# Gates and norm sums by quarters of the tokens, an up projection written in another order, later merges and a root on ScalarE

## The chip, the core and the metric

The kernel runs on one core of one Trainium2 chip. A core has several engines that run at the same time, each through its own list of instructions: TensorE (PE in the profile, with PEld for its weight loads), VectorE (DVE), ScalarE (ACT), GpSimd (POOL) and SyncE (SP), whose queue issues most of the transfers (DMA) here. PE multiplies and accumulates into PSUM, in banks of 128 partitions by 512 f32 numbers. The metric is the device time of one execution in microseconds (us), as the median of several runs.

## The reference, cut to what matters

One layer of a decoder for 1024 tokens and 1024 channels: a first norm, one input projection for two mixers (a gated delta rule with a causal convolution, and dilated window attention), the output projection, a second norm, a gated MLP with a causal convolution, and a last norm.

```python
def rmsnorm(x, w):
    xf = x.astype(jnp.float32)
    y = xf * lax.rsqrt(jnp.mean(xf * xf, axis=-1, keepdims=True) + EPS)
    return (y * w.astype(jnp.float32)).astype(x.dtype)
...
    h = rmsnorm(x, norm1_w)
    proj = h @ w_in
    qkv_a, z_a, b_a, a_a, qkv_b = (...)
    beta = jax.nn.sigmoid(b_a)
    g = -jnp.exp(a_log) * jax.nn.softplus(a_a + dt_bias)
    o_a = gated_delta_rule(qa, ka, va, g, beta)     # unit lower triangular solves of 64 x 64
    o_b = dilated_attention(qb, kb, vb)
    x = x + jnp.concatenate([o_a, o_b], axis=-1) @ w_out
    h = rmsnorm(x, norm2_w)
    u = causal_dwconv(h @ w_up, ffn_conv_w)
    gate, up = u[..., :D_FF], u[..., D_FF:]         # D_FF = 2816
    x = x + (jax.nn.silu(gate) * up) @ w_down
    return rmsnorm(x, final_norm_w)
```

`b_a` and `a_a` are the eight columns of the projection that hold the gates (four heads each). A norm's root is one number for each token; the kernel multiplies with it behind a product, so a product can run before the root is known.

## The kernel before

All large tensors lie transposed: channels on the 128 partitions, tokens along the free axis. A factor of a product is split into a high part (`hi`, rounded) and the rest (`lo`), and a product of two such factors is three matmuls, hi by hi, lo by hi and hi by lo (`mm3`, line 204). One of them is 128 x 128 weights by 512 tokens.

The order of PE's instructions is the order in which the program calls `mm` (line 191), which stamps each with a running number. That order is made by a small planner, `Weave` (lines 26 to 120). It holds a modelled clock of PE and a modelled time at which each tile is ready. The stages are generators with a rank; each yields the time that it would have to wait, and the planner runs the first in rank whose time has come. `wv.need(tile, slack=s)` is the modelled wait for that tile, lengthened by `s` us; `next_bank` is the same for a bank of PSUM. Where no stage of higher rank is due, the next split product of the projections (25 tiles of 16 split products beside the first 48) fills the place. The other engines follow the order in which the program issues to them, within what a scheduler rearranges by priority and by the `after(...)` lines, which only set an order; `uv` is VectorE with high priority.

The stages that the change touches:

- `first` (line 359), the first product: three tiles of keys, 48 split products, as the eight channel tiles of x arrive. `norms` (373) and `gates` (399) are woven into it. `acc` holds the squares of x summed over the channel tiles; eight matmuls with `ones` sum it over partitions, a column for each 128 tokens. VectorE scales the sums and GpSimd raises them to the power -1/2 (`rsqrt`, 239), giving `rst`. Transposes on PE (line 196) spread it over all partitions, and VectorE copies it into `rstdB`. The gates: `wba`, the weights of the eight gate columns padded to 32, is used in two batches of eight matmuls over 512 tokens, in which the channel tile modulo 4 sets one of four column groups of PE. ScalarE copies the rows into `barow`, and eight matmuls with the selection matrix `sel` add the four groups and turn the tokens to partitions. In the trace an f32 matmul leaves two records.
- `forward_sub` and `merges` (715): the inverses of the triangular matrices. VectorE makes blocks of 32 by substitution, which go through memory (`xdram`) into block-diagonal tiles `x`; `merges` joins them to 64 and 128 with small matmuls of `x` with `um`, two pairs of heads one after the other.
- the up projection (`up`, line 1300): 22 tiles, each with seven block products P1 to P7 of a Strassen kind, four split products each (k = 0 to 3). The factors are blocks of weights (A11, S1 to S4, A12, A22; two of them in one `pair`) and of activations (B11, T1 to T4, B21, B22, one for each k). P1, P6, P7 and P4 accumulate in one bank, `pa`; between them ScalarE copies it out (`p1`, `u2`, `u3`), and the product behind must wait for the copy. In the first tile `before` is None: there `rms2_power` (1226) sums the squares of the second norm, held in `rstdB` by then, with eight matmuls with `ones`. `up_weights` (1252) splits the weights of the next tiles.
- `final_norm` (1579), called for three pieces of the tokens; its last call has `more`, squares that join late. Scaling on VectorE and the power on GpSimd stand between its sums and its spread.

## Time and profile before

| what | number |
|---|---|
| median of three runs | 1202.09 us (1201.26 to 1202.52) |
| profiled execution | 1200.62 us |
| its span, first to last instruction | 1198.7 us |
| around the span | 1.92 us |
| granted TensorE clock, mean | 0.997 |
| VectorE, ScalarE, GpSimd busy | 964.7, 572.8 and 53.1 us |
| read and written in memory | 117.68 and 38.03 MB |

The stages follow each other in the span: the first product and gates up to about 45 us, projections with the delta rule and the attention to 467 us, the output projection to 555 us, the up projection to 977 us, the down projection to 1187 us, and the last norm. In a row of the timeline the first number is the start in us, the second the duration or, for a group of equal instructions, the time from the first start to the last end; then engine, line, operation, output and inputs, shapes and count, and in brackets how long the engine had been idle and what ended that. The durations of PE's rows overlap, since matmuls are pipelined: the pace is read from the starts. In a row of windows come the stretch, its length, busy time and count of PE, PEld, VectorE, ScalarE and GpSimd, and then the granted clock, the share of the DMA engines and GB/s.

### The profile page before, as it was taken

Reading aid. Unit: us, or ns where it says so; the run is one execution under the profiler, and the core shown is the slowest. Engines: PE = TensorE matmul, PEld = TensorE weight load, DVE = VectorE, ACT = ScalarE, POOL = GpSimd, SP = SyncE. Lnnn points to the kernel's source line nnn. Section 1 sums busy time; section 2 is a strip of 40 time slices with the busy share of each in tenths; the row PEclk is TensorE's granted clock in tenths of the full one; section 3 lists DMA queues with packets and bytes.
Section 4 is the critical chain, followed back from the end, with each engine's and each line's share of the span. In section 5 each row is a group of like instructions: output and inputs, shape, how many; then the busy total and the mean of one; then the engine's idle time right before and its main releaser. Section 6 shows DMA issues by size and latency. Waiting matters only on the chain.

```text
span 1198.7 us, 18255 instructions
## 1 busy us (share of the span) xinstructions
PE 1186.9 (99%) x6994; PEld 981.9 (82%) x6994; DVE 964.7 (80%) x1540; ACT 572.8 (48%) x1121; POOL 53.1 (4%) x50
## 2 busy tenths in 40 slices
PE   9999999999999999999999999999999999999997
PEld 7888888898777778888888888888888888888887
DVE  7686996484577787777898988989888889898987
ACT  7383343363343444555454544445454454445452
POOL 0212001014000000000000000000000000000001
PEclk9999999999999999999999999999999999999999
DMA  7323356737543314443223223131322396356724
GB/s 237 106 75 103 106 138 160 213 105 209 170 127 105 98 37 126 164 147 117 74 69 104 82 77 106 53 106 55 104 87 71 100 378 215 114 181 219 242 98 158
DMA packets 114664, 156.91 MB, mean 131 GB/s; under 512 B 54512, under 2 KB 65552, under 8 KB 114576
## 3 DMA queue, kind: packets, MB, share of 16 engines
q1 hardware_dynamic: 113856, 155.21, 40.7%
q8 instruction: 55, 0.90, 0.3%
q10 hardware_dynamic: 720, 0.53, 0.1%
q14 instruction: 33, 0.27, 0.1%
HBM read 117.68 MB, written 38.03 MB: 130 GB/s over the span
## 4 chain that ended last, share of the span: by engine, by line
PE 91%; DVE 3%; DMA 2%; ACT 2%; issue 1%; SPq 1%; POOL 0%; DVEq 0%; ACTq 0%; POOLq 0%
PE ps L192 41%; PE pa L192 20%; PE dw L192 17%; PE pc L192 10%; PE ps L201 1%; PE ps L196 1%; DMA vdram<-vT 1%; SPq L139 1%; DVE vT L139 1%; DMA xdram<-xi 1%; ACT sm L141 1%; DMA wst<-in_wu 0%; PE warm L192 0%; DMA vtok<-vdram 0%; DVE x1h L139 0%
## 5 line engine op out<-in xcount | busy, mean ns | idle before, releaser
L192 PE MATMUL dw<-pr 128*128 128x512 f32 (+1 forms) x984 | 211.4, 376 | 0.0
L192 PEld LDWEIGHTS dw<-pr 128*128 128x128 f32 x984 | 176.7, 188 | 33.7
L192 PE MATMUL ps<-xhi,whi 128*128 128x512 f32 x448 | 184.7, 412 | 0.0
L192 PE MATMUL ps<-xhi,wlo 128*128 128x512 f32 x448 | 175.6, 392 | 0.0
L192 PE MATMUL ps<-xlo,whi 128*128 128x512 f32 x448 | 175.5, 392 | 0.0
L192 PE MATMUL pa<-T,pair 128*128 128x512 f32 x528 | 127.1, 390 | 0.2
L192 PEld LDWEIGHTS pa<-T,pair 128*128 128x128 f32 x528 | 98.9, 188 | 21.2 <-ACT u L139 0.7
L192 PEld LDWEIGHTS ps<-xhi,whi 128*128 128x128 f32 x448 | 84.9, 189 | 19.7 <-issue 3.6
L192 PEld LDWEIGHTS ps<-xhi,wlo 128*128 128x128 f32 x448 | 84.5, 189 | 18.5
L192 PEld LDWEIGHTS ps<-xlo,whi 128*128 128x128 f32 x448 | 84.8, 189 | 14.5
L139 ACT ACTIVATE u<-pa 128x512 f32<-128x512 f32 x44 | 26.3, 599 | 109.7 <-PE pa L192 109.7
L139 DVE SCALAR_TENSOR_TENSOR y<-xu,fcw,y 128x1023 f32<-128x1023 f32 (+1 forms) x44 | 56.3, 1280 | 24.4 <-ACT y L139 24.4
L139 ACT ACTIVATE pr<-wd 128x1024 fp32r<-128x1024 f32 x33 | 35.0, 1060 | 74.6 <-DVE wd L139 36.9
L139 ACT ACTIVATE whi<-wst 128x1024 fp32r<-128x1024 f32 (+2 forms) x38 | 38.5, 1013 | 56.3 <-PE ps L192 47.1
L192 PE MATMUL pa<-B,A 128*128 128x512 f32 x264 | 63.5, 389 | 0.0
L192 PE MATMUL pa<-T,S 128*128 128x512 f32 x264 | 63.4, 389 | 0.0
L192 PE MATMUL pc<-T,S 128*128 128x512 f32 x264 | 63.4, 389 | 0.0
L192 PE MATMUL pc<-B,pair 128*128 128x512 f32 x264 | 63.4, 389 | 0.0
L139 DVE TENSOR_TENSOR wst<-wst 128x512 f32<-128x512 f32 x88 | 60.3, 685 | 0.7
L192 PE MATMUL ps<-B,pair 128*128 128x512 f32 x252 | 60.5, 389 | 0.0
L141 ACT ACTIVATE sm<-sm,mx 128x128 f32<-128x128 f32 (+7 forms) x64 | 35.4, 555 | 51.4 <-DVE mx L141 51.4
L192 PEld LDWEIGHTS pa<-T,S 128*128 128x128 f32 x264 | 49.5, 188 | 10.3
(243 smaller groups left out, 2238.9 us busy)
## 6 DMA issues: line engine op xcount, KB each, us to landing
wst<-in_wu SPq DMA_DIRECT2D x44, 512.0 KB, 3.7
wd<-in_wd SPq DMA_DIRECT2D x44, 512.0 KB, 4.5
wst<-in_wi SPq DMA_DIRECT2D x25, 512.0 KB, 4.0
upark<-y SPq DMA_DIRECT2D x22, 512.0 KB, 3.6
r<-upark SPq DMA_DIRECT2D x22, 512.0 KB, 9.5
wa<-in_wd SPq DMA_DIRECT2D x22, 256.0 KB, 3.0
apark<-aqkv SPq DMA_DIRECT2D x8, 512.0 KB, 4.4
wst<-in_wo SPq DMA_DIRECT2D x8, 512.0 KB, 3.6
```

What stands on the lines that cost most here:

```text
L139: return getattr(eng, op)(*a, **kw)
L141: return getattr(eng, op)(*a, **kw)
L192: tc.stamp_issue_order_token(nc.tensor.matmul(dst, lhs, rhs, start=start, stop=stop, **kw).ins, TOKEN)
L196: tc.stamp_issue_order_token(nc.tensor.transpose(dst, src, ident).ins, TOKEN)
L201: tc.stamp_issue_order_token(nc.tensor.transpose(dst, src[rows], ident[rows, rows]).ins, TOKEN)
```

## The change

The two batches of gate matmuls become one of 32: for each channel tile, each of the four column groups takes a quarter of the tokens (`by_quarter`, 256 tokens in runs of 32). So no group has to be added to another. `pick`, 32 columns with ones in column 8, adds the sum of `acc` to the same bank, and one transpose of VectorE brings gates and sum to `bat`, tokens on partitions. `barow`, its copies and `sel` are gone. The spread of the root and the decay's bank have more slack.

The second norm's sums in the up projection are formed in the same way. P2 of its first tile is issued in other pieces, and a split of the second tile's A11 is placed behind the copy `u2`. `merges` asks for its tiles with slack 4.5 in place of 2.5. In the last call of `final_norm` ScalarE makes the square root and VectorE the reciprocal; a small square root at step 20 of the down projection, `sc(mark, eps, AF.Sqrt)`, has ScalarE load the table for that there.

```diff
--- before.py
+++ after.py
@@ -233,6 +233,8 @@
     sa.dma_start(n1, I["n1"])
     mhalf = const("mhalf", [P, NCH])
     ve.memset(mhalf, -0.5)
+    eps = const("eps", [P, 1])
+    ve.memset(eps, EPS)
     phalf = const("phalf", [P, NCH])
     ve.memset(phalf, 0.5)
 
@@ -339,15 +341,15 @@
     ve.memset(ones, 1.0)
     tri = tile_(sp, [P, P], F32, "tri", "r0", 1)
     sy.dma_start(tri, I["tri"])
-    sel = const("sel", [P, 8], I["sel"])
+    pick = const("pick", [P, 32])
+    ve.memset(pick, 0.0)
+    ve.memset(pick[:, 8:9], 1.0)
     gcw = const("gcw", [P, 12, 4], I["gcw"])
     gnw = const("gnw", [P, 1], I["gnw"])
     alog = const("alog", [P, H], bass.AP(tensor=I["a_log"].tensor, offset=I["a_log"].offset, ap=[[0, P], [1, H]]))
     dtb = const("dtb", [P, H], bass.AP(tensor=I["dt_bias"].tensor, offset=I["dt_bias"].offset, ap=[[0, P], [1, H]]))
     gw2 = const("gw2", [P, 1])
     ve.tensor_scalar(gw2, gnw, 0.5, None, op0=OP.mult)
-    barow = A("barow", "go")
-
 
     wbank = bank("atr", "warm")
     for _ in range(10):
@@ -370,17 +372,27 @@
     rst = const("rst", [P, NCH])
     rstdB = const("rstdB", [P, S])
 
+    def by_quarter(t):
+        return t.rearrange("p (c g i) -> p g c i", g=4, i=32)
+
+    bat = sp.tile([P, NCH, 32], F32, name="bat")
+
     def norms():
+        yield wv.need(wba, xts[-1], slack=4.0)
+        pt = yield from next_bank("atr", wba, xts[-1])
+        for k in range(KT):
+            for g in range(4):
+                o = 32 * g
+                mm(pt[o:o + 32, :256], wba[:, k, :], by_quarter(xts[k])[:, g], 0.107, k == 0, False, tile_position=(0, o))
         yield wv.need(acc, slack=8.0)
-        ssp = yield from next_bank("atr", acc)
-        for c in range(NCH):
-            mm(ssp[:, c:c + 1], acc[:, c * P:(c + 1) * P], ones[:, :1], 0.215)
-            if c % 2:
-                yield APART
-        ve.tensor_scalar(rst, ssp[:, :NCH], 1.0 / 1024, EPS, op0=OP.mult, op1=OP.add)
+        for g in range(4):
+            o = 32 * g
+            mm(pt[o:o + 32, :256], pick, by_quarter(acc)[:, g], 0.107, False, True, tile_position=(0, o))
+        uv.transpose(bat.rearrange("p c j -> p (c j)"), pt[:, :256])
+        uv.tensor_scalar(rst, bat[:, :, 8], 1.0 / 1024, EPS, op0=OP.mult, op1=OP.add)
         rsqrt(rst, rst, NCH)
         wv.done.add("rst")
-        yield wv.need(rst)
+        yield wv.need(rst, slack=4.0)
         for h in range(2):
             if h:
                 yield wv.need(rstdB, slack=0.3)
@@ -398,24 +410,9 @@
 
     def gates():
 
-        yield wv.need(wba, xts[-1], slack=4.0)
-        for h in range(2):
-            pt = yield from next_bank("atr", wba, xts[-1])
-            for k in range(KT):
-                o = 32 * (k % 4)
-                mm(pt[o:o + 32], wba[:, k, :], xts[k][:, half(h)], 0.23, k < 4, k >= 4, tile_position=(0, o))
-            ac.activation(barow[:, half(h)], pt, AF.Copy)
-            yield 2 * APART
-        yield wv.need(barow, slack=2.0)
-        pt = yield from next_bank("atr", barow)
-        for c in range(NCH):
-            mm(pt[:, c * 8:(c + 1) * 8], barow[:, c * P:(c + 1) * P], sel, 0.215)
-            if c % 2:
-                yield APART
         yield from wv.until("rst")
         ba = sp.tile([P, NCH, 8], F32, name="ba")
-        ve.tensor_tensor(ba, pt[:, :64].rearrange("p (c j) -> p c j", c=NCH),
-                                rst[:, :, None].to_broadcast([P, NCH, 8]), op=OP.mult)
+        ve.tensor_tensor(ba, bat[:, :, :8], rst[:, :, None].to_broadcast([P, NCH, 8]), op=OP.mult)
         ac.activation(beta, ba[:, :, :H], AF.Exp, scale=-1.0)
         ve.tensor_scalar(beta, beta, 1.0, None, op0=OP.add)
         ve.reciprocal(beta, beta)
@@ -431,7 +428,7 @@
         g = sp.tile([P, NCH, H], F32, name="g")
         ve.scalar_tensor_tensor(g, az, -1.0, ea[:, None, :].to_broadcast([P, NCH, H]), op0=OP.mult,
                                        op1=OP.mult)
-        pt = yield from next_bank("atr", g)
+        pt = yield from next_bank("atr", g, slack=1.5)
         g32 = g.rearrange("p c h -> p (c h)")
         mm(pt[:, :NCH * H], tri, g32, 0.215)
         mm(pt[:NCH * H, P:2 * P], g32, tri, 0.215)
@@ -739,7 +736,7 @@
             return t.rearrange("p (h c j) -> p h c j", h=2, c=NCH)
 
         w1ps = [bank(t) for t in tags]
-        yield wv.need(*w1ps, *x64s, *ys, slack=2.5)
+        yield wv.need(*w1ps, *x64s, *ys, slack=4.5)
         for h, y, x64, e in heads:
             for c in range(NCH):
                 for a, b in halves:
@@ -1211,6 +1208,7 @@
             split_block(hblock("T2", i), b11)
             split_block(hblock("B21", i), b21)
             split_block(hblock("T3", i), b12)
+            last["t3"] = last["hi"]
             ve.tensor_tensor(b21, b21, b11, op=OP.subtract)
             split_block(hblock("T4", i), b21)
             last["lasts"] = [last["hi"]]
@@ -1225,10 +1223,12 @@
 
     def rms2_power():
         ps = bank("atr")
-        for c in range(NCH):
-            mm(ps[:, c:c + 1], rstdB[:, c * P:(c + 1) * P], ones[:, :1], 0.215)
+        for g in range(4):
+            o = 32 * g
+            mm(ps[o:o + 32, :256], pick, by_quarter(rstdB)[:, g], 0.107, tile_position=(0, o))
         rs = sp.tile([P, NCH], F32, name="rs")
-        uv.tensor_scalar(rs, ps[:, :NCH], 1.0 / 1024, EPS, op0=OP.mult, op1=OP.add)
+        uv.transpose(bat.rearrange("p c j -> p (c j)"), ps[:, :256])
+        uv.tensor_scalar(rs, bat[:, :, 8], 1.0 / 1024, EPS, op0=OP.mult, op1=OP.add)
         rsqrt(rs, rs, NCH)
         return rs
 
@@ -1265,6 +1265,8 @@
                 for name in ("A11", "S2", "S1"):
                     w[name] = block(name, "Xb")
             split_block(w["A11"], g0)
+            if n == 1:
+                after(last["hi"], last["u2"], "the last channels go first")
             ve.tensor_tensor(g0, g0, u0, op=OP.subtract)
             ve.tensor_tensor(u0, u0, u1, op=OP.add)
             split_block(w["S1"], u0)
@@ -1311,21 +1313,22 @@
 
             yield from up_product(n, "P5", pc, True, False)
             pd = bank("hf", "pd")
-            yield from up_product(n, "P2", pd, ks=range(3))
+            yield from up_product(n, "P2", pd, ks=(0,))
         yield from up_product(n, "P6", pa, False, False)
         u2 = tile_(wp, [P, 512], F32, "u2", "wlo", 2)
-        inst = ac.activation(u2, pa, AF.Copy)
+        last["u2"] = inst = ac.activation(u2, pa, AF.Copy)
         if before is None:
             for hi in last["lasts"]:
                 after(hi, inst, "the next product waits for the copy")
         if before is None:
             rs = rms2_power()
+            yield from up_product(n, "P2", pd, False, False, ks=(1,))
         else:
             yield from up_product(n, "P5", pc, True, False)
         yield from up_product(n, "P7", pa, False, False)
         if before is None:
 
-            yield from up_product(n, "P2", pd, False, ks=(3,))
+            yield from up_product(n, "P2", pd, False, ks=(2, 3))
         else:
             pd = yield from next_bank("hf")
             yield from up_product(n, "P2", pd)
@@ -1586,8 +1589,12 @@
                 mm(ss[:, c:c + 1], t[:, c * P:(c + 1) * P], ones[:, :1], 0.215, i == 0 and c == 0,
                    i == len(parts) - 1, skip_group_check=True)
         rs = tile_(sp, [P, 4], F32, "rs3", "rs3", 2)
-        inst = ve.tensor_scalar(rs[:, :n_], ss[:, :n_], 1.0 / 1024, EPS, op0=OP.mult, op1=OP.add)
-        rsqrt(rs[:, :n_], rs[:, :n_], n_)
+        if more:
+            ac.activation(rs[:, :n_], ss[:, :n_], AF.Sqrt, scale=1.0 / 1024, bias=eps)
+            ve.reciprocal(rs[:, :n_], rs[:, :n_])
+        else:
+            inst = ve.tensor_scalar(rs[:, :n_], ss[:, :n_], 1.0 / 1024, EPS, op0=OP.mult, op1=OP.add)
+            rsqrt(rs[:, :n_], rs[:, :n_], n_)
         if hh:
 
             keep("vector", inst)
@@ -1663,6 +1670,8 @@
             ahead = n + 1 + (stage == 3)
             if ahead < len(STEPS):
                 prep(*STEPS[ahead], JOBS.get(n, ()))
+            if n == 20:
+                sc(mark, eps, AF.Sqrt)
             if (stage, j) == (3, HT - LAST - 2):
                 outs = final_norm(1, whole, ("hf", "ch"), lambda: down_step(stage, j))
             elif stage < 3 or j < HT - LAST:
```

PE in the first product. A row is an operation by its tiles, the shape of its output, and how many of a kind stand in a row; `ps` is a bank of PSUM, `xhi`, `xlo`, `whi` and `wlo` are the parts of x and of the weights. Before, from the second half of the sums on:

```order
L192 MATMUL ps<-ones,acc 128x1 x2
L192 MATMUL ps<-sel,barow 128x8 x2
L192 MATMUL ps<-xhi,whi 128x512
L192 MATMUL ps<-xlo,whi 128x512
L192 MATMUL ps<-xhi,wlo 128x512
L192 MATMUL ps<-ones,acc 128x1 x2
L192 MATMUL ps<-sel,barow 128x8 x2
L192 MATMUL ps<-xhi,whi 128x512
```

And after, around the sums:

```order
L192 MATMUL ps<-xhi,whi 128x512
L192 MATMUL ps<-xlo,whi 128x512
L192 MATMUL ps<-xhi,wlo 128x512
L192 MATMUL ps<-acc,pick 32x256 x4
L192 MATMUL ps<-xhi,whi 128x512
L192 MATMUL ps<-xlo,whi 128x512
L192 MATMUL ps<-xhi,wlo 128x512
```

The `sel` matmuls are gone and the sums stand in one piece. The gate batch ahead of them was two rows of 32x512 x8 and is one:

```order
L192 MATMUL ps<-xlo,whi 128x512
L192 MATMUL ps<-xhi,wlo 128x512
L192 MATMUL ps<-xt,wba 32x256 x32
L192 MATMUL ps<-xhi,whi 128x512
L192 MATMUL ps<-xlo,whi 128x512
```

It stands behind the same split product (the 22nd) as the first batch did.

PE at the merges, with the numbers of the tiles; `qT,kT` are the last products of the delta rule's preparation, `x64,um` the first of `merges`. Before:

```order
L192 MATMUL ps_1934<-qT_1772,kT_604 128x128 x4
L192 MATMUL ps_1924<-xhi_140,whi_1778 128x512
L192 MATMUL ps_1924<-xlo_141,whi_1778 128x512
L192 MATMUL ps_1924<-xhi_140,wlo_1779 128x512
L192 MATMUL ps_1734<-x64_1706,um_683 32x32 x16
L192 MATMUL ps_1734<-x64_1706,um_804 32x32 x16
```

And after:

```order
L192 MATMUL ps_1927<-xhi_155,whi_1781 128x512
L192 MATMUL ps_1927<-xlo_156,whi_1781 128x512
L192 MATMUL ps_1927<-xhi_155,wlo_1782 128x512
L192 MATMUL ps_1927<-xhi_167,whi_1781 128x512
L192 MATMUL ps_1927<-xlo_168,whi_1781 128x512
L192 MATMUL ps_1927<-xhi_167,wlo_1782 128x512
L192 MATMUL ps_1927<-xhi_179,whi_1781 128x512
L192 MATMUL ps_1927<-xlo_180,whi_1781 128x512
L192 MATMUL ps_1927<-xhi_179,wlo_1782 128x512
L192 MATMUL ps_1737<-x64_1709,um_686 32x32 x16
L192 MATMUL ps_1737<-x64_1709,um_807 32x32 x16
```

Four split products instead of one stand between them now; three of the four are shown.

PE in the first tile of the up projection, from P2 (`pd`) over P6 (`T,S`), the sums and P7 (`T,pair` into `pa`) to the start of P4. Before:

```order
L192 MATMUL pd<-B_5741,pair 128x512 x3
L192 MATMUL pa<-T_5406,S_5922 128x512 x3
L192 MATMUL pa<-T_5572,S_5922 128x512 x3
L192 MATMUL pa<-T_5738,S_5922 128x512 x3
L192 MATMUL pa<-T_5900,S_5922 128x512 x3
L192 MATMUL ps<-ones,rstdB 128x1 x8
L192 MATMUL pa<-T_5412,pair 128x512 x3
L192 MATMUL pa<-T_5578,pair 128x512 x3
L192 MATMUL pa<-T_5744,pair 128x512 x3
L192 MATMUL pa<-T_5906,pair 128x512 x3
L192 MATMUL pd<-B_5903,pair 128x512 x3
L192 MATMUL pa<-T_5416,pair 128x512 x3
```

And after:

```order
L192 MATMUL pd<-B_5412,pair 128x512 x3
L192 MATMUL pa<-T_5409,S_5925 128x512 x3
L192 MATMUL pa<-T_5575,S_5925 128x512 x3
L192 MATMUL pa<-T_5741,S_5925 128x512 x3
L192 MATMUL pa<-T_5903,S_5925 128x512 x3
L192 MATMUL ps<-rstdB,pick 32x256 x4
L192 MATMUL pd<-B_5578,pair 128x512 x3
L192 MATMUL pa<-T_5415,pair 128x512 x3
L192 MATMUL pa<-T_5581,pair 128x512 x3
L192 MATMUL pa<-T_5747,pair 128x512 x3
L192 MATMUL pa<-T_5909,pair 128x512 x3
L192 MATMUL pd<-B_5744,pair 128x512 x3
```

P2's first piece is one split product long instead of three, its second stands between the sums and P7, and the last two, of which one row is shown, stand between P7 and P4.

More of the change, by code (lines that the diff above doesn't have):

```diff
@@ L1754, in host_inputs @@
         "ident": np.eye(128, dtype=np.float32),
-        "sel": np.array([[p % 32 == j for j in range(8)] for p in range(128)], np.float32),
         "tri": (j[:, None] <= j[None, :]).astype(np.float32),
```

## The prediction

> **What bounds the kernel now.** I read the busy shares first, then the shares of the chain that ended last, then all waits of PE, then the stretches that the diff touches, engine by engine.

> ```profile
> PE 1186.9 (99%) x6994; PEld 981.9 (82%) x6994; DVE 964.7 (80%) x1540; ACT 572.8 (48%) x1121; POOL 53.1 (4%) x50
> PE 91%; DVE 3%; DMA 2%; ACT 2%; issue 1%; SPq 1%; POOL 0%; DVEq 0%; ACTq 0%; POOLq 0%
> PE ps L196 <- POOL rs L139: 1.1, 1, 1.1
> PE ps L192 <- DMA x<-xdram: 1.1, 1, 1.1
> PE ps L192 <- ACT w L141: 0.7, 2, 0.5
> PE ps L201 <- DVE sm L141: 0.6, 2, 0.3
> ```

> PE is busy 99% of the span and carries 91% of the last chain; its waits (the last four rows: total us, times, longest) are short. So time falls in two ways only: PE gets less work, or one of its few waits goes. Both kinds are in this diff. The profiled execution took 1200.62 us, of which 1198.7 is the span and 1.92 lies around it. The sums below are made against it; the median of the runs, 1202.09, is 1.47 higher, and I carry that difference over. Runs span 1201.26 to 1202.52, so 0.2% (2.4 us) is about what can be told from no change.

> **Front: gates and norm sums (gain 3.25 us).** PE has no idle time between these rows:

> ```profile
> 20.80 0.39 PE L192 MATMUL ps<-xhi,wlo 128*128 128x512 f32 x1
> 21.12 1.92 PE L192 MATMUL ps<-xt,wba 128*32 128x512 f32 x16
> 24.57 0.64 PE L192 MATMUL ps<-xt,wba 128*32 128x512 f32 x4
> 28.60 0.50 PE L192 MATMUL ps<-ones,acc 128*128 128x1 f32 x4
> 34.52 0.51 PE L192 MATMUL ps<-sel,barow 128*128 128x8 f32 x4
> 37.04 0.60 PE L196 MATMUL ps<-ident,rst 128*128 128x128 f32 x4
> 562.17 2.89 PE L192 MATMUL pa<-T,S 128*128 128x512 f32 x12
> 564.89 1.84 PE L192 MATMUL ps<-ones,rstdB 128*128 128x1 f32 x16
> ```

> The last two rows give the pace of a full 128x512 matmul: 12 of them from 562.17 to 564.89, 2.72/12 = 0.227 us, a split product of three 0.68. From the end of the product at 20.80 (21.03) to the first spread transpose at 37.04 lie 16.01 us, in which the order places 12 split products, 12 x 0.68 = 8.16. The extras are the other 7.85. From one gate batch's start to the other's are 3.45, with two split products (1.36) in between, so a batch costs 2.09 (two: 4.18); the ones and sel matmuls, each piece with its changes of kind, take the remaining 3.67.

> After, the gate batch is 32 matmuls of 256 tokens. An f32 matmul leaves two records (8 matmuls, x16), so 64 records; four column groups run side by side: the first four records of the second batch last 0.64 (its row is cut there), all 16 of the first 1.92, so a further round costs (1.92 - 0.64)/3 = 0.43, and 2.09 less 1.72 leaves 0.37 for the changes of kind. At half the width a round is 0.215 and 16 rounds are 3.44; with 0.37 they cost 3.81. The four pick matmuls are 8 records, two rounds, 0.43 + 0.37 = 0.80. Together 4.6, against 7.85: 3.25 gained. The streaming of the gates itself is not cheaper (3.44 before and after); what goes is the sel and ones work.

> The unknown is whether short records overlap as well and whether reading tokens in runs of 32 out of 128 costs.

> ```profile
> L192 PE MATMUL ps<-kT,qT 64*128 64x128 f32 x16 | 2.0, 322 | 0.0
> L192 PE MATMUL ps<-kT,qT 64*32 64x128 f32 x64 | 1.7, 269 | 0.0
> L139 DVE STREAM_TRANSPOSE vT<-vT 128x1024 f32<-128x1024 f32 x4 | 4.9, 1236 | 0.0
> 33.47 0.17 DVE L139 TENSOR_SCALAR rst<-ps 128x8 f32<-128x8 f32 x1 [1.09 <-PE ps L192]
> 33.72 1.64 POOL L139 TENSOR_TENSOR rst<-rst,mhalf 128x8 f32<-128x8 f32 x1 [32.67 <-DVE rst L139]
> ```

> The first two rows are the nearest to that: 128 tokens read strided (32 keys, 269 ns) are no longer than contiguous (322 ns). Bounds: the gain is 3.25 if all overlaps; with the 18 rounds a half longer (5.8, and 0.74) 1.3; with rounds as long as now (18 x 0.43 = 7.7, and 0.74) it is a loss of 0.6. I take the upper end.

> [...]

> What follows the sums: the transpose of 128x256 on DVE is an estimated 0.31 (a quarter of 1.236), the root's scaling 0.17, POOL's power 1.64. The sums leave PE at about 29.5; on DVE the transpose stands behind one weight split of 1.2, so the root is there near 34.3. The order now has the first spread six split products later (behind the 40th instead of the 34th), at 21.03 + 18 x 0.68 + 4.6 = 37.9: covered by some 3.5 us. The gates' own chain of some 3 us behind the root is ready near 37.3, its first product stands behind that spread. If this cover is gone, it costs its excess, under 1.

> **Merges (gain 2.2 us).**

> ```profile
> 198.04 1.41 PE L192 MATMUL ps<-x,um 32*32 32x32 f32 x66
> 200.53 1.50 PE L192 MATMUL ps<-x,um 32*32 32x32 f32 x62 [1.09 <-DMA x<-xdram]
> 201.96 0.80 PE L192 MATMUL ps<-xhi,whi 128*128 128x512 f32 x1
> 204.64 0.40 PE L192 MATMUL ps<-xhi,whi 128*128 128x512 f32 x1
> 200.00:202.00 2.00, 1.47 (x63) 1.41 (x63) 1.66 (x5) 0.00 (x0) 0.00 (x0) 0.79 0.45 70
> 202.00:204.00 2.00, 2.00 (x6) 1.61 (x6) 0.70 (x1) 0.59 (x1) 0.00 (x0) 0.50 0.46 75
> 176.36 0.69 DVE L139 TENSOR_TENSOR xr<-ps,rstdB 128x512 f32<-128x512 f32 x1 [0.49 <-PE ps L192]
> ```

> PE waits 1.09 for the second head's blocks, and directly behind it the granted clock is 0.50 (seventh number of the window rows, after PE, PEld, DVE, ACT and POOL): six 128x512 matmuls take 201.96 to 204.64 = 2.68 instead of 1.36. The price of this place is 1.09 + 1.32 = 2.4. After, three more split products (2.04) stand ahead of the first merge product. The blocks' copies through memory hang on DVE's substitution, which itself waits for PE (176.36), so I let them move with the front by 3.25: ready at 197.3, while PE asks at 198.04 - 3.25 + 2.04 + 1.41 = 198.2. The wait goes, with 1 us to spare, and with it the drop in clock. I take 2.2, with 0.2 for what PE still loses at its start. Bounds: nothing gained if the copies do not move with PE (asked at 198.2, ready at 200.5: a wait of 2.3 and the half clock again, a loss of about 1.2). The moved products come out of the later fill: the order has them three ahead at every later place and 14 of 448 left behind the last attention values instead of 16, so the fill does not run out.

> **Middle (0, within 1.7).** The chain and the attention are woven differently now. PE's waits there are the 0.7 and 0.6 above and four shorter ones; about 1.7 in all with their starts. They can go, move or double; I take nothing.

> **Up projection, first tile (gain 1.55 us).**

> ```profile
> 554.69 2.88 PE L192 MATMUL pa<-B,A 128*128 128x512 f32 x12
> 566.88 3.02 PE L192 MATMUL pa<-T,pair 128*128 128x512 f32 x12
> 570.65 3.06 PE L192 MATMUL pa<-T,pair 128*128 128x512 f32 x12
> 574.34 2.99 PE L192 MATMUL pa<-B,A 128*128 128x512 f32 x12
> 565.71 0.63 ACT L139 ACTIVATE S<-wst 128x512 fp32r<-128x512 f32 x1 [2.20 <-DVE wst L139]
> 566.25 0.58 ACT L139 ACTIVATE u<-pa 128x512 f32<-128x512 f32 x1
> ```

> The tile takes 554.69 to 574.34 = 19.65. Six products are 16.32. Of the other 3.33, the ones stretch has 564.89 to 566.88 = 1.99 (sixteen records, then PE waits for the copy of pa, which ACT starts only at 566.25 behind a split); 566.88 + 2.72 + 0.68 = 570.28 against 570.65 is 0.37 of waiting for the next copy; 570.65 + 2.72 to 574.34 is 0.97 for the root's spread, which stays. After: pick 0.80 in place of the ones, two places where parts of P2 cover a copy (0.80 + 0.68 = 1.48 over 0.58 and its hops; 1.36 over the next), spread 0.97: 16.32 + 0.80 + 0.97 = 18.1. The A11 split of the next tile, which waited for its load at the head of ACT's line, now stands behind the copy. P6 comes 1.36 earlier and its last T block is due near 562.9; without that split ahead it is made near 560.3. The root has transpose, scaling and 1.64 of POOL to do, ready near 568, needed at the end of P4 near 571.7. Bounds: if the copy still ends at 566.83, one more part of P2 stands behind P7 and the gain is a loss of 0.3 (0.68 less the 0.37); if the pick costs only its 0.43, 1.9.

> **End (gain 0.55 us).**

> ```profile
> 1191.21 0.16 DVE L139 TENSOR_SCALAR rs<-ps 128x2 f32<-128x2 f32 x1
> 1191.52 0.70 POOL L139 TENSOR_TENSOR rs<-rs,mhalf 128x2 f32<-128x2 f32 x1 [6.73 <-DVE rs L139]
> 1192.27 0.65 PE L196 MATMUL ps<-ident,rs 128*128 128x128 f32 x4 [1.09 <-POOL rs L139]
> L139 ACT ACTIVATE ge<-gel 128x8 f32<-128x8 f32 x4 | 0.9, 220 | 0.0
> L141 DVE RECIPROCAL mx<-mx 128x2 f32<-128x2 f32 x32 | 5.3, 165 | 4.0 <-ACT sm L141 3.4
> L139 ACT ACT_TABLE_LOAD x5 | 6.4, 1283 | 8.5 <-DVE qT L139 7.3 <-PEq L1767 1.2
> 1090.09 1.06 ACT L139 ACTIVATE pr<-wd 128x1024 fp32r<-128x1024 f32 x1 [2.60 <-DVE wd L139]
> ```

> PE waits 1.09 for scaling, POOL and hops. After: a small ScalarE operation 0.22, a reciprocal 0.165, hops as now about 0.15: 0.54. The new table load (1.28) stands in the down projection, where ACT is idle 2.60 ahead of 1090.09; it is hidden. If it fell ahead of the root instead, this part would lose 0.7.

> **The sum.** 3.25 + 2.2 + 0 + 1.55 + 0.55 = 7.55, less 0.05 for the new memset ahead of the warm-up: 7.5. Profiled execution 1193.1, median 1202.09 - 7.5 = 1194.6.

> **Rivals.** (a) The merges' wait stays or moves to the copies behind: that term is nothing or a loss of 1.2, so 1196.8 to 1198.0. For it: the copies pass through memory, and 1 us of spare is little. Against it: DVE waits for PE ahead of them. (b) The wait goes and the half clock stays, because the 32x32 matmuls of 198 to 202 are themselves little work: 1.3 less gain, 1195.9. The row at 202.00 shows half clock after only 1.09 of idleness. [...] (c) The reshuffled middle adds a wait over 1 us and a half clock: 2.5 back, 1197.1. (d) The other side: strided quarters do not run side by side. The 18 rounds of gates and pick (3.9 as summed) stretch; the kernel gets slower than before from 7.5 more, 2.9 times as long, and four records in a row instead of side by side would be four times, 11.6 more: 1206.2. Against it: four at once in 0.43 now, and the strided row. (e) Parts of the diff change nothing at PE, the up passage for one: 1196.2.

> **Chances.** All terms about as summed 0.50; (b) or (e) 0.22; (a) 0.11; (c) 0.11; (d) or something like it 0.06. Up to (c) all are faster by over 2.4, but for a few that add up: faster 0.91, same 0.05, slower 0.04. The likeliest case lies within 1193 to 1196. The range holds (a) and (c) and a gain in the middle: 1192.0 to 1198.8.

> **What would show it.** Front: one gate batch of about 3.7, one row of four picks, the first spread near 37.9 with no wait of PE. Merges: no wait for the blocks and a clock of 1.00 in the two windows behind. Up: tile from P1 to P1 18.1. End: PE's wait 0.5 for DVE. It is wrong if the gate batch takes 6 or more, if a wait over 1 us appears at the merges or the middle, or if a table load stands ahead of the last root.

## The result, and the profile after

The changed kernel takes 1192.24 us (median of 6 runs, 1191.63 to 1192.62) against 1201.14 of the kernel before beside it (6 runs, 1199.89 to 1202.52): a ratio of 0.9925, 95% interval 0.9912 to 0.9938. So it is 8.9 us faster, where 7.5 were forecast; 1192.24 lies just inside the range of 1192.0 to 1198.8. Larger sets of runs of the kernel before spread over 5.6 to 7 us, those of the changed one over 1 to 1.6; the experiments show a part of the reason. Beside the experiments the kernel before has medians of 1200.68, 1200.30 and 1200.28 (11, 12 and 27 runs), so against them the gain is rather 8.0 to 8.4.

The head of the profile page after, and PE's longest waits behind the start:

```profile
span 1189.8 us, 18253 instructions
PE 1180.1 (99%) x6994; PEld 975.9 (82%) x6994; DVE 965.4 (81%) x1545; ACT 573.2 (48%) x1122; POOL 54.6 (5%) x49
PE ps L196 <- DVE rs L139: 0.7, 1, 0.7
PE ps L192 <- ACT w L141: 0.5, 1, 0.5
PE ps L192 <- DVE ct L141: 0.4, 1, 0.4
```

The wait for the merges' blocks (1.1) is not in the list any more, and the last root's is 0.7 in place of 1.1. PE is busy for the same 99% of a shorter span.

The timeline of the first product after, on PE, VectorE and GpSimd:

```profile
20.29 0.39 PE L192 MATMUL ps<-xhi,wlo 128*128 128x512 f32 x1
20.60 3.66 PE L192 MATMUL ps<-xt,wba 128*32 128x256 f32 x64
24.20 0.50 PE L192 MATMUL ps<-xhi,whi 128*128 128x512 f32 x1
28.50 0.64 PE L192 MATMUL ps<-acc,pick 128*32 128x256 f32 x8
37.37 0.60 PE L196 MATMUL ps<-ident,rst 128*128 128x128 f32 x4
...
29.72 0.44 DVE L141 STREAM_TRANSPOSE bat<-ps 128x256 f32<-128x256 f32 x1
32.18 1.64 POOL L139 TENSOR_TENSOR rst<-rst,mhalf 128x8 f32<-128x8 f32 x1 [31.14 <-DVE rst L141]
```

64 records take 3.66: sixteen rounds of four side by side, as summed. The root is there at 33.82 and its first spread comes at 37.37, so 3.5 us of cover are left.

The merges after, PE's timeline and then the stretches around (the granted clock is the third number from the end):

```profile
195.93 0.39 PE L192 MATMUL ps<-xhi,wlo 128*128 128x512 f32 x1
196.25 2.21 PE L192 MATMUL ps<-x,um 32*32 32x32 f32 x128
198.39 0.50 PE L192 MATMUL ps<-xhi,whi 128*128 128x512 f32 x1
...
196.00:198.00 2.00, 2.00 (x112) 1.75 (x112) 0.80 (x4) 0.50 (x1) 0.00 (x0) 1.00 0.42 66
198.00:200.00 2.00, 2.00 (x37) 1.70 (x31) 1.53 (x3) 1.51 (x3) 0.00 (x0) 1.00 0.45 72
200.00:202.00 2.00, 2.00 (x11) 1.65 (x10) 2.00 (x3) 0.23 (x1) 0.00 (x0) 1.00 0.63 94
```

All 128 records of the small matmuls stand in one piece of 2.21; before they were two pieces of 1.41 and 1.50 with the wait between. The clock stays at 1.00. The blocks come through memory in eight copies; their issues, on the queue of SyncE, before and then after (durations, then the starts of the first and the last):

```profile
L139 SPq DMA_DIRECT2D x<-xdram x8: 319/487/491, 189.9 to 198.4; - x8
L139 SPq DMA_DIRECT2D x<-xdram x8: 319/486/490, 185.8 to 194.3; - x8
```

The last copy is issued 4.1 earlier; the 48th split product starts 3.8 earlier (47.55 and 43.75). So the copies moved with PE.

The first tile of the up projection after, on PE, and ScalarE's copies and splits in it:

```profile
547.84 2.88 PE L192 MATMUL pa<-B,A 128*128 128x512 f32 x12
556.77 0.64 PE L192 MATMUL ps<-rstdB,pick 128*32 128x256 f32 x8
557.34 0.96 PE L192 MATMUL pd<-B,pair 128*128 128x512 f32 x3
558.14 2.90 PE L192 MATMUL pa<-T,pair 128*128 128x512 f32 x12
565.75 3.01 PE L192 MATMUL pa<-B,A 128*128 128x512 f32 x12
...
556.88 0.60 ACT L139 ACTIVATE u<-pa 128x512 f32<-128x512 f32 x1 [3.10 <-PE pa L192]
558.41 0.62 ACT L139 ACTIVATE A<-wst 128x512 fp32r<-128x512 f32 x1
```

The copy u2 starts as soon as P6 ends, while PE has the pick and a part of P2 to do; the tile takes 547.84 to 565.75 = 17.91. The split of A11 comes behind.

The end after: ScalarE's root, VectorE's reciprocal, PE's spread, and the early table load:

```profile
1182.72 0.26 ACT L139 ACTIVATE rs<-ps,eps 128x2 f32<-128x2 f32 x1 [0.76 <-PE ps L192]
1183.02 0.17 DVE L139 RECIPROCAL rs<-rs 128x2 f32<-128x2 f32 x1 [0.39 <-ACT rs L139]
1183.33 0.62 PE L196 MATMUL ps<-ident,rs 128*128 128x128 f32 x4 [0.70 <-DVE rs L139]
...
1078.10 1.28 ACT L139 ACT_TABLE_LOAD   x1
1081.62 1.06 ACT L139 ACTIVATE pr<-wd 128x1024 fp32r<-128x1024 f32 x1 [1.08 <-DVE wd L139]
```

ScalarE still waits 1.08 behind the table load, so that load is hidden.

Where the 8.9 us of span went, from the starts of the same PE instructions in the two traces (each stretch before less the same stretch after):

| stretch | before | after | gain | forecast |
|---|---|---|---|---|
| start to the 22nd split product | 20.35 | 19.83 | 0.52 | -0.05 |
| first product with gates and sums, 22nd to 48th | 27.20 | 23.92 | 3.28 | 3.25 |
| on to the last product of queries and keys ahead of the merges | 149.58 | 149.56 | 0.02 | 0 |
| merges, with the same four split products | 8.20 | 5.08 | 3.12 | 2.2 |
| middle, to the up projection | 349.36 | 349.45 | -0.09 | 0 |
| its first tile | 19.65 | 17.91 | 1.74 | 1.55 |
| the rest to the last spread | 618.30 | 617.93 | 0.37 | 0.55 |
| behind the start of the last matmul | 6.1 | 6.2 | -0.1 | 0 |

The sum is 8.9. The split product behind the merges starts 0.12 slower than one in a row of its kind. This falls into the row of the merges before, and into the row of the middle after, so 0.12 of the 3.12 belongs to the middle, which is then even.

### The profile page after: what moved, and what is told of

Same layout as the page of the kernel before. It is cut to its first block, busy times and chain, and to the rows that moved or that the text cites. A ratio compares the mean times of both kernels' runs of the same rounds, so it can differ in the third digit from the quotient of the medians.

```text
span 1189.8 us, 18253 instructions
## 1 busy us (share of the span) xinstructions
PE 1180.1 (99%) x6994; PEld 975.9 (82%) x6994; DVE 965.4 (81%) x1545; ACT 573.2 (48%) x1122; POOL 54.6 (5%) x49
## 4 chain that ended last, share of the span: by engine, by line
PE 97%; DVE 1%; ACT 0%; issue 0%; DVEq 0%; ACTq 0%
PE ps L192 47%; PE pa L192 20%; PE dw L192 18%; PE pc L192 10%; PE ps L201 1%; PE ps L196 1%; PE warm L192 0%; DVE x1h L139 0%; ACT sm L141 0%; DVE sm L141 0%; PE pd L192 0%; DVE avt L139 0%; DVE aqkv L139 0%; DVE wke L141 0%; DVE ct L141 0%
## 5 line engine op out<-in xcount | busy, mean ns | idle before, releaser
L192 PE MATMUL dw<-pr 128*128 128x512 f32 (+1 forms) x984 | 211.4, 376 | 0.0
L192 PEld LDWEIGHTS dw<-pr 128*128 128x128 f32 x984 | 176.7, 188 | 33.7
L192 PE MATMUL ps<-xhi,whi 128*128 128x512 f32 x448 | 183.7, 410 | 0.0
L192 PE MATMUL ps<-xhi,wlo 128*128 128x512 f32 x448 | 175.2, 391 | 0.0
L192 PE MATMUL ps<-xlo,whi 128*128 128x512 f32 x448 | 174.9, 391 | 0.0
L192 PE MATMUL pa<-T,pair 128*128 128x512 f32 x528 | 126.8, 389 | 0.0
L192 PEld LDWEIGHTS pa<-T,pair 128*128 128x128 f32 x528 | 99.1, 188 | 20.6
L192 PEld LDWEIGHTS ps<-xhi,whi 128*128 128x128 f32 x448 | 84.2, 188 | 18.9 <-issue 2.7
L192 PEld LDWEIGHTS ps<-xhi,wlo 128*128 128x128 f32 x448 | 84.1, 188 | 18.3
L192 PEld LDWEIGHTS ps<-xlo,whi 128*128 128x128 f32 x448 | 84.4, 188 | 14.9 <-DVE xlo L139 0.3
L139 ACT ACTIVATE u<-pa 128x512 f32<-128x512 f32 x44 | 26.4, 599 | 114.4 <-PE pa L192 114.4
L139 DVE SCALAR_TENSOR_TENSOR y<-xu,fcw,y 128x1023 f32<-128x1023 f32 (+1 forms) x44 | 56.4, 1281 | 22.1 <-ACT y L139 22.0
L139 ACT ACTIVATE pr<-wd 128x1024 fp32r<-128x1024 f32 x33 | 35.0, 1061 | 73.4 <-DVE wd L139 35.8
L192 PE MATMUL pa<-B,A 128*128 128x512 f32 x264 | 63.5, 389 | 0.0
L192 PE MATMUL pc<-B,pair 128*128 128x512 f32 x264 | 63.4, 389 | 0.0
L192 PE MATMUL pc<-T,S 128*128 128x512 f32 x264 | 63.4, 389 | 0.0
L192 PE MATMUL pa<-T,S 128*128 128x512 f32 x264 | 63.4, 389 | 0.0
L139 DVE TENSOR_TENSOR wst<-wst 128x512 f32<-128x512 f32 x88 | 60.4, 686 | 0.8
L139 ACT ACTIVATE whi<-wst 128x1024 fp32r<-128x1024 f32 (+2 forms) x38 | 38.5, 1013 | 46.5 <-PE ps L192 38.9
L192 PE MATMUL ps<-B,pair 128*128 128x512 f32 x252 | 60.5, 389 | 0.0
L141 ACT ACTIVATE sm<-sm,mx 128x128 f32<-128x128 f32 (+7 forms) x64 | 35.5, 556 | 49.7 <-DVE mx L141 49.7
L192 PEld LDWEIGHTS pa<-T,S 128*128 128x128 f32 x264 | 49.6, 188 | 10.3
```

Source lines behind the costliest of these rows:

```text
L139: return getattr(eng, op)(*a, **kw)
L141: return getattr(eng, op)(*a, **kw)
L192: tc.stamp_issue_order_token(nc.tensor.matmul(dst, lhs, rhs, start=start, stop=stop, **kw).ins, TOKEN)
```

## The experiments

Times below are medians of the runs with their range. The changed kernel, run again beside the second group, gives 1192.09, so 1192.2 is its base. The first and the third group have no run of the changed kernel beside them, but the medians of the kernel before given above agree to 0.4 between the three groups. Resampling the runs gives 95% intervals of some 0.3 to 0.8 us either way for a difference from the base, and of nearly 2 us where the runs spread over 4.

**One part undone at a time.** First the front: `norms` and `gates` as before, with `barow` and `sel`, all else as changed.

```diff
-        for k in range(KT):
-            for g in range(4):
-                o = 32 * g
-                mm(pt[o:o + 32, :256], wba[:, k, :], by_quarter(xts[k])[:, g], 0.107, k == 0, False, tile_position=(0, o))
...
+            for k in range(KT):
+                o = 32 * (k % 4)
+                mm(pt[o:o + 32], wba[:, k, :], xts[k][:, half(h)], 0.23, k < 4, k >= 4, tile_position=(0, o))
```

> The changed kernel with norms and gates of the first product as before (two gate batches, ones, barow, sel). Theory, by the starts of PE's rows in the two traces: the front is worth 3.3 us, so this is 5.6 us faster than the kernel before (the whole change: 8.9), and the wait at the merges stays away, since the blocks' copies move with PE. Rival: the front is worth more than its own stretch, because the merges' copies don't move with PE or the middle is woven differently; then this differs from the kernel before by less than 4.5 or more than 6.5 us, and the missing time lies behind 45 us of the span.

Measured: 1195.28 (1194.99 to 1195.54), 3.1 slower than the changed kernel. In its trace the stretch from the 22nd to the 48th split product is 27.20 again, every later stretch agrees with the changed kernel's within 0.25 (most of it in the last spread, in which the clock dropped at 1186.78), and no wait for the merges' blocks is there. So the front is worth its own stretch and nothing else, and the wait stays away without it.

Then the merges alone undone:

```diff
-        yield wv.need(*w1ps, *x64s, *ys, slack=4.5)
+        yield wv.need(*w1ps, *x64s, *ys, slack=2.5)
```

> The changed kernel with the merges' slack back at 2.5. Theory: PE waits 1.1 us for the second blocks again, the granted clock is about 0.5 in the 3 us behind, and the two halves of the merge products fall apart; together 3.0 us, so this is 5.9 us faster than the kernel before. Rival: it was the new order of the chain and the attention (other fill, other stalls) that gave part of it: then the stretch up to the first products of 64x64 loses about 2.2 only, and the rest is found between 210 and 460 us.

Measured: 1194.99 (1193.01 to 1196.86), 2.8 slower, with runs 3.9 apart. PE in its trace:

```profile
194.57 1.26 PE L192 MATMUL ps<-x,um 32*32 32x32 f32 x66
196.47 1.19 PE L192 MATMUL ps<-x,um 32*32 32x32 f32 x62 [0.64 <-DMA x<-xdram]
197.59 0.50 PE L192 MATMUL ps<-xhi,whi 128*128 128x512 f32 x1
```

Here the wait is 0.64, the clock stayed at 1.00, and the stretch is 6.12, 1.04 over the changed kernel's. The mean clock of its six runs lies between 0.998 (1193.0 and 1193.3) and 0.995 (1196.7 and 1196.9). So the wait has a price of about 1 us without the half clock, and a larger one with it, in some executions only: the two runs at 0.998 are 0.8 and 1.0 slower than the changed kernel, the two at 0.995 are 4.5 and 4.6. Neither theory had that: both took the half clock for certain.

The two pieces take 1.26 + 1.19 = 2.45 here, 0.24 more than the one piece of 2.21, all at full clock. This is what the interruption itself costs beside the wait.

The up projection's passage undone (ones for the sums, P2 in three parts and one, no line for A11):

```diff
-            mm(ps[o:o + 32, :256], pick, by_quarter(rstdB)[:, g], 0.107, tile_position=(0, o))
+            mm(ps[:, c:c + 1], rstdB[:, c * P:(c + 1) * P], ones[:, :1], 0.215)
...
-                after(last["hi"], last["u2"], "the last channels go first")
...
-            yield from up_product(n, "P2", pd, False, False, ks=(1,))
```

> The changed kernel with the up projection's first tile as before (ones for the sums, P2 in three parts and one, the split of A11 not held behind the copy). Theory: the tile takes 19.6 us from P1 to P1 instead of 17.9, this is 7.2 us faster than the kernel before. Rival: without that order the later tiles make up for it or lose more; then the difference isn't seen in the first tile alone but at the start of the third.

Measured: 1194.90 (1193.37 to 1197.32), 2.7 slower, runs 4 apart. The profiled execution has the tile at 19.32, 1.41 over the changed kernel's, and nothing made up later (the next tile is as long in both). The theory's 1.7 is short of the measured 2.7. The three runs at a mean clock of 0.998 take 1193.4 to 1194.0, the three at 0.997 take 1195.8 to 1197.3; whether these hold a half clock isn't shown, since the profile is of one of the first.

The last root undone:

```diff
-            ac.activation(rs[:, :n_], ss[:, :n_], AF.Sqrt, scale=1.0 / 1024, bias=eps)
-            ve.reciprocal(rs[:, :n_], rs[:, :n_])
+            inst = ve.tensor_scalar(rs[:, :n_], ss[:, :n_], 1.0 / 1024, EPS, op0=OP.mult, op1=OP.add)
+            rsqrt(rs[:, :n_], rs[:, :n_], n_)
...
-                sc(mark, eps, AF.Sqrt)
```

> The changed kernel with the last root made by VectorE's scaling and GpSimd's power as before, and no early load of a table. Theory: PE's wait ahead of the last spread is 1.09 instead of 0.70, this is 8.5 us faster than the kernel before. Rival: the early table load costs time in the down projection, and this is as fast as the changed kernel (8.9) or faster.

Measured: 1192.80 (1192.55 to 1193.71), 0.6 slower, with ranges that overlap; its profile has PE's 1.09 back. The early table load costs nothing that shows. This profile is of the longest of the six runs, and two of PE's waits in it are not in the changed kernel's profiles:

```profile
PE ps L192 <- ACT ot L139: 0.6, 1, 0.6
PE ps L192 <- ACT sq L141: 0.5, 1, 0.5
```

The clock is at 1.00 up to 1186.28, and yet the stretches ahead of the merges and behind them, which the edit doesn't touch, are 0.76 and 0.80 longer than in the changed kernel's profile. So executions differ by more than the clock.

**What in the up passage it is.** The changed kernel again, and three kernels that undo one piece of the passage each: the sums, the pieces of P2, and the line that holds the split of A11 back.

> The changed kernel again, as the base for the next three. Both theories: within 0.6 us of 1192.24, the runs within 1.2 us of each other; the kernel before spread over several us on the same chip.

Measured: 1192.09 (1191.70 to 1193.34), 0.15 from the first set. The runs lie 1.6 apart, a little more than the 1.2 expected.

```diff
-        for g in range(4):
-            o = 32 * g
-            mm(ps[o:o + 32, :256], pick, by_quarter(rstdB)[:, g], 0.107, tile_position=(0, o))
+        for c in range(NCH):
+            mm(ps[:, c:c + 1], rstdB[:, c * P:(c + 1) * P], ones[:, :1], 0.215)
```

> The changed kernel with only the second norm's sums as before: eight matmuls with ones, the rest of the passage new. Theory: the ones take about 1.0 us beyond the 0.57 that the pick stretch has, as the copy u2 is covered by the P2 part behind; 0.5 to 1.0 slower than the changed kernel, runs close together since PE doesn't wait. Rival: it is the thin matmuls with ones that halve the clock in some executions: then the runs spread over 3 us or more, as they did with the whole passage as before.

Measured: 1193.42 (1192.58 to 1194.01), 1.3 slower; the tile is 18.95 in its trace, 1.03 longer than in the changed kernel. No half clock is in its profile, and no run is below 0.997: the sixteen records of the ones matmuls, 1.84 us without a wait, brought none here.

```diff
-            yield from up_product(n, "P2", pd, ks=(0,))
+            yield from up_product(n, "P2", pd, ks=range(3))
...
-            yield from up_product(n, "P2", pd, False, ks=(2, 3))
+            yield from up_product(n, "P2", pd, False, ks=(3,))
```

> The changed kernel with only P2's pieces as before (k 0 to 2 ahead of P6, k 3 behind P7). Theory: PE waits 0.2 to 0.3 for u2 and 0.3 for u3, 0.5 slower than the changed kernel, and no spread. Rival: short waits are what halves the clock by chance: then the runs spread over 3 us.

Measured: 1192.88 (1192.25 to 1193.40), 0.8 slower, with ranges that overlap; the tile is 18.47, 0.55 longer. The runs lie 1.2 apart.

```diff
-            if n == 1:
-                after(last["hi"], last["u2"], "the last channels go first")
```

> The changed kernel without the line that holds the split of A11 behind the copy u2. Theory: that split waits for its load at the head of ScalarE's line, the last T and B blocks come 1.5 to 2.3 us later, and S stands ahead of u2: PE waits for P6's last block and for u2, 0.5 to 1.5 slower, with runs that spread by 2 us or more where the waits halve the clock. Rival: P2's parts cover it all: within 0.2 us of the changed kernel.

Measured: 1194.14 (1193.12 to 1197.99), 2.0 slower, and this profile caught the half clock. ScalarE, PE and two stretches:

```profile
556.77 0.63 ACT L139 ACTIVATE A<-wst 128x512 fp32r<-128x512 f32 x1 [4.67 <-DMA wst<-in_wu]
558.35 0.61 ACT L139 ACTIVATE T<-hb 128x512 fp32r<-128x512 f32 x1
561.70 0.58 ACT L139 ACTIVATE u<-pa 128x512 f32<-128x512 f32 x1
...
557.97 0.50 PE L192 MATMUL pa<-T,S 128*128 128x512 f32 x1 [1.12 <-ACT T L139]
562.33 5.07 PE L192 MATMUL pa<-T,pair 128*128 128x512 f32 x12 [0.65 <-ACT u L139]
...
560.00:562.00 2.00, 1.68 (x7) 0.83 (x3) 2.00 (x4) 0.84 (x2) 0.00 (x0) 0.50 0.00 0
564.00:566.00 2.00, 2.00 (x6) 1.52 (x6) 1.87 (x4) 1.57 (x2) 1.02 (x1) 0.50 0.00 0
```

The split of A11 stands 4.67 us at the head of ScalarE's line until its load has landed (3.05 for the same wait in the first profile of the kernel before); the last T blocks and u2 stand behind it. PE waits for T blocks and for u2, the clock halves for about 7 us, and the tile takes 23.60. This is the longest of the seven runs; the other six, at 0.998, are 1.0 to 2.8 slower than the changed kernel. So without the line every run is slower than the median of the base, and one of seven has the half clock; with the line none of the profiles has a half clock in this tile. That the same happens in the old passage is not shown: there P6 starts 1.36 later, and PE waits for u2 alone. The sums and P2's pieces bring 1.03 and 0.55 in the profiles. The three medians add to 4.1, more than the 2.7 of the whole passage, so the pieces are not independent.

**Where the spread of the kernel before comes from.** The kernel before again, for a second profile of it.

> The kernel before once more, for a second profiled execution of it. Theory: it has two places in which PE waits among thin matmuls, the merges and the first tile of the up projection, and each halves the clock in some executions only. So the runs spread from about 1196.8 to 1203.7, the mean granted clock falls from 0.998 to 0.994 with the time, and in this profile the stretches at half clock lie at these two places or at none. Rival: the spread comes from somewhere else, such as transfers; then this profile differs from the first in a stretch with a clock of 1.00.

Measured: 1199.36 (1196.66 to 1203.53, 11 runs). Its profile, in the same views as the first:

```profile
197.47 1.26 PE L192 MATMUL ps<-x,um 32*32 32x32 f32 x66
199.40 1.19 PE L192 MATMUL ps<-x,um 32*32 32x32 f32 x62 [0.67 <-DMA x<-xdram]
564.16 4.61 PE L192 MATMUL pa<-T,pair 128*128 128x512 f32 x12 [0.20 <-ACT u L139]
...
200.00:202.00 2.00, 2.00 (x42) 1.71 (x37) 1.55 (x3) 0.59 (x1) 0.00 (x0) 1.00 0.44 75
564.00:566.00 2.00, 1.84 (x5) 1.47 (x6) 1.97 (x5) 2.00 (x5) 0.10 (x1) 0.68 0.00 0
566.00:568.00 2.00, 2.00 (x6) 1.59 (x5) 2.00 (x3) 0.69 (x1) 1.84 (x1) 0.50 0.00 0
```

The same kernel, and the half clock has changed places: none at the merges (stretch 6.14 instead of 8.20), but one in the first tile of the up projection (21.26 instead of 19.65). That is what the theory had forecast, and of these eleven runs those with a mean clock of 0.994 are the longest (1203.4 and 1203.5), those with 0.998 among the shortest (1196.7 to 1198.1).

The mean clock has to be read with care. In every profile the clock falls to half a few us ahead of the end, somewhere in the last 3.8 to 7.5 us of the span. So a run without any other drop reads 0.997 or 0.998, and a drop of 3.4 us takes another 0.0014 (3.4 / 2 / 1196). Both profiles of the kernel before, each with one drop, read 0.997; so does the changed kernel's second profile, with none before 1183.24. By these figures a run at 0.996 or less holds another drop, one at 0.998 holds none, and one at 0.997 can be either.

The merges' slack alone on the kernel before:

```diff
-        yield wv.need(*w1ps, *x64s, *ys, slack=2.5)
+        yield wv.need(*w1ps, *x64s, *ys, slack=4.5)
```

> The kernel before with the merges' slack at 4.5 and nothing else. Theory: the wait and the lottery of the merges go, that of the up projection stays: fastest about 1.0 under the kernel before's fastest, median 2 to 3 lower, spread 4 instead of 7. Rival: the wait goes only because the other parts move the transfers; then this is within 0.5 of the kernel before and the wait for the blocks is in the profile.

Measured: 1197.60 (1196.40 to 1199.02, 11 runs) against 1200.28 (27 runs): 2.7 less, a ratio of 0.9979 with interval 0.9971 to 0.9988. The wait is gone without the other parts, so the slack alone does it. But the fastest run is only 0.3 under the fastest of the kernel before, not 1.0, and the spread is 2.6, not 4. No run is below 0.997, so none holds more than one drop of 3.4 us, and the five at 0.998 hold none. These five alone lie between 1196.4 and 1197.8, and the kernel before's at 0.998 between 1196.7 and 1199.0. A part of the spread is thus not the clock. What it is was not settled. Candidates are waits that differ by execution: for A11's load on ScalarE (2.37 to 3.11 in the old passage), for the merges' blocks (0.67 and 1.09 in the two profiles of the kernel before), and those in the middle of the profile of the last root undone.

Merges and up passage together on the kernel before:

```diff
-        yield wv.need(*w1ps, *x64s, *ys, slack=2.5)
+        yield wv.need(*w1ps, *x64s, *ys, slack=4.5)
...
-            mm(ps[:, c:c + 1], rstdB[:, c * P:(c + 1) * P], ones[:, :1], 0.215)
+            mm(ps[o:o + 32, :256], pick, by_quarter(rstdB)[:, g], 0.107, tile_position=(0, o))
...
+            if n == 1:
+                after(last["hi"], last["u2"], "the last channels go first")
```

> The kernel before with the merges' slack and the up projection's passage changed, front and last root as before. Theory: the terms add, 1192.1 + 3.3 for the front + 0.5 for the root = 1195.9, and both lotteries are gone, spread 1.5 or less. Rival: the kernel before in its fastest executions (1196.8) is almost there already, so the terms don't add: then it is 1194.5 or less, or 1196.5 or more.

P2's pieces are changed too (not shown). Measured: 1195.42 (1194.99 to 1196.70, 5 runs). The terms add, to within 0.5; the spread is 1.7 where 1.5 or less was expected.

At last a longer wait: the changed kernel with the merges' slack at 0.5.

```diff
-        yield wv.need(*w1ps, *x64s, *ys, slack=4.5)
+        yield wv.need(*w1ps, *x64s, *ys, slack=0.5)
```

> The changed kernel with the merges' slack at 0.5: the merge products stand two split products (1.4 us) earlier than with 2.5, so PE waits some 2.0 us for the second blocks. Theory: the longer the wait, the more executions have the clock halved: all or nearly all of them, 1192.1 + 2.0 + 0.4 + 1.5 to 3 = 1196 to 1197.5, spread 2 or less. [...]

Measured: 1197.61 (1195.52 to 1199.44, 10 runs), eight of the ten at a mean clock of 0.995 or less. PE's wait and a stretch of its profile:

```profile
PE ps L192 <- DMA x<-xdram: 2.8, 2, 1.7
200.00:202.00 2.00, 2.00 (x8) 1.71 (x7) 1.15 (x5) 0.00 (x0) 0.00 (x0) 0.50 0.50 73
```

With this longer wait nine of the ten runs are at 0.996 or less, and so hold another drop by the figures above, as the theory had it: only one, at 0.997, may have none. The wait is 2.8 where the theory had 2.0, in two parts of 1.71 and 1.12, both for the second pair's blocks, and the median lies 0.1 above its bound. The spread is 3.9, as it was with a slack of 2.5, and not the theory's 2.

## Why the prediction was right

**Front, forecast 3.25, measured 3.28.** Each step held: rounds of 0.215 (the first eight records take 0.64, all 64 take 3.66: 3.02 for 14 rounds), no cost of strided tokens, and the changes of kind (3.68 from the end of the product ahead, 20.52, to the next product at 24.20, and some 0.1 in that product's own slower start, where 3.81 was summed). Rival (d), records in a row, is out: 64 in 3.66 where 64 of 0.215 in a row would be 13.8.

The root was forecast near 34.3 and came at 33.82, but that is luck. The terms that the prediction names (29.5, 1.2, 0.31, 0.17 and 1.64) add to 32.8 and a few hops. What took the rest is a second weight split: the transpose started at 29.72 and took 0.44 where 0.31 was estimated, and then VectorE was idle for 0.63 and made another split ahead of the scaling:

```profile
30.79 1.23 DVE L139 TENSOR_TENSOR wlo<-wst,whi 128x1024 fp32r<-128x1024 f32 x1 [0.63 <-ACT whi L139]
31.93 0.16 DVE L141 TENSOR_SCALAR rst<-bat 128x8 f32<-128x8 f32 x1
```

The cover took that, so it cost nothing.

**Merges, forecast 2.2, measured 3.12 in this pair of profiles.** The mechanism held and the term was too small. The sum had the wait and the half clock, 2.4, less 0.2. It took the pieces of 1.41 and 1.50 as given, but in one piece they are 2.21. Of these 0.7, 0.24 is the interruption itself, as the two profiles with the pieces at full clock show (1.26 and 1.19). The other 0.46 is a gap of 0.15 within the first piece, ahead of its last two records, and 0.31 in the second piece, of which the part behind 201.17 ran at half clock. The sum counted that clock only for the six full matmuls behind. (The blocks waited for are those of the second pair of heads, not of the second head.) Rival (a) is out: the copies' issues moved with PE, and the wait is gone. Rival (b), that the half clock comes from the thin work alone, is out for this length: none of the profiles without that wait has it.

What the forecast could not see from one profile is that the half clock was a matter of chance. It was counted at the merges, where it happened to be, and not in the up projection, where it happened not to be. With two profiles of the kernel before (1200.62 and 1199.36) it was one place each time. So it is luck that the sum came near the medians: single runs of the kernel before lie between 1196.7 and 1203.7, that is 4.4 to 11.5 above the changed kernel's median, and a profile with no half clock or with two would have given another sum.

**Up projection, forecast 1.55, measured 1.74**. The old passage took 19.3 to 21.3 in the profiles here, the new one 17.9 in all. The steps held, with the pick at 0.57 from its start to the next product's, and 0.12 in that product's slower start, in place of 0.80.

**End, forecast 0.55, measured 0.37 to the last spread.** The operations were sized right (0.26 and 0.17); what was too small is the hops: PE's wait of 0.70 holds 0.27 of them, where 0.15 was taken.

**Start and middle.** The 0.5 of the start is no part of the change: the 22nd split product begins anywhere between 19.75 and 20.77 in the profiles here, of kernels that hardly differ up to it. The 0.05 taken for the new memset is shown by no run: PE's first matmul starts at 1.13 after and 1.11 before. Rival (c) is out: the middle is even, to 0.1. The forecast of 7.5 came out 1.4 low because of the merges (0.9), the start (0.5) and the up projection (0.2), less the end (0.2).

## What to carry to other kernels

A short wait of a busy TensorE can cost more than its length: here a wait of 0.64 cost another 0.24 at full clock, and in some executions a half clock behind it costs more (1.32 behind the wait of 1.09 in the first profile of the kernel before: six full matmuls in 2.68 in place of 1.36). So add what the interruption costs the work around it, and ask whether it lies among thin matmuls, as that one did. Where repeated runs of a kernel spread by more than a per mille, compare each run's mean clock, and take a second profile before a stretch is priced: one profile shows one draw. Put work that waits for a load behind work that is ready, where the engine takes them in that order (here a split stood 4.67 at the head of ScalarE's line, ahead of the last T blocks and u2).

## What the runs showed of the hardware

By its records in the traces the granted clock had these stretches, among others:

```
kernel before, first profile     half clock from 201.17 to 204.58    3.413 us
kernel before, second profile    half clock from 564.72 to 568.13    3.413 us
split of A11 not held back       half clock from 559.93 to 566.76    6.827 us
merges' slack 0.5                half clock from 196.06 to 202.88    6.827 us
changed kernel, first profile    full clock from 5.02 to 1186.03     1181.011 us
```

PE was not idle all through the 3.413 us ahead of these drops. In the first profile of the kernel before they held 0.3 us of a full product, 106 of the 128 small records of the merges and the wait of 1.09, in its second 0.8 us of P6, the sixteen records of the ones matmuls, a wait of 0.20 and the start of P7. The one piece of 2.2 us of small matmuls without a wait brought no drop in any of the ten profiles that have it. The pieces of 1.26 and 1.19 with the wait of 0.64 between them, in the profile with the merges undone, brought none either. What decides between a drop and none was not measured.
